# Latent attention of the decoded rows computed among the latents, inside the last pair's list

## The chip, the cores and the metric

The kernel runs on one core of one Trainium2 chip. A core has five engines with their own instruction queues: TensorE (PE: matrix products and transposes into PSUM), VectorE (DVE), ScalarE (ACT), GpSimd (POOL) and SyncE (SP, which here only starts DMAs). The metric is device time in microseconds, from the start of the program to its end. All arithmetic is to be exact to about single precision.

## The reference, cut to what matters

The program is one layer of an encoder with two attention branches, a gated merge and a convolutional feed-forward part, for a prompt of 1024 rows and, with the same weights, for 32 new rows of another sequence ("sample") that has a cache of 512 past rows. The change concerns branch A, the latent attention, of the sample alone:

```python
D_MODEL = 1024; SEQ = 1024; DEC_SEQ = 32; PAST_LEN = 512
H_A = 8; NOPE = 64; ROPE = 32; DV = 64; Q_RANK = 384; KV_RANK = 256

def expand_latent(c_kv, w_uk, w_uv):
    B, S, _ = c_kv.shape
    return (c_kv @ w_uk).reshape(B, S, H_A, NOPE), (c_kv @ w_uv).reshape(B, S, H_A, DV)

def mla_attend(q_nope, q_rope, qpos, k_nope, k_rope, v, kpos):
    s = (jnp.einsum('bqhd,bshd->bhqs', q_nope, k_nope)
         + jnp.einsum('bqhr,bsr->bhqs', q_rope, k_rope)).astype(jnp.float32) * MLA_SCALE
    mask = (kpos[None, :] // CHUNK) <= (qpos[:, None] // CHUNK)
    p = jax.nn.softmax(jnp.where(mask, s, NEG), axis=-1)
    return jnp.einsum('bhqs,bshd->bqhd', p.astype(v.dtype), v)

# for the sample:
    k_nope, v_a = expand_latent(jnp.concatenate([past_ckv, c_kv], axis=1), w_uk, w_uv)
    o_a = mla_attend(q_nope, q_rope, pos, k_nope, jnp.concatenate([past_krope, k_rope], axis=1), v_a, kpos)
```

So 544 latent rows of 256 numbers (512 cached, 32 new) are expanded to keys and values of 8 heads by 64, and each of 32 queries attends to all of them in each head. Since keys are latents times w_uk, the scores are also (query times the transpose of w_uk) times latents, and the output is also (weights times latents) times w_uv: both orders give the same numbers.

## The kernel before

The stages run in this order: normalisation and adaptive scales, branch B (stage_sb), the latents (stage_lat), branch A (stage_mla), the merge, the feed-forward part. Outside stage_mla's lists a scheduler of the framework decides at build time in which order the instructions of an engine stand.

Precision: most products are made of three (mm3, L70): both factors are split into a high and a low part of type float32r ("hi" on ACT, L64, "lo" on DVE, L67), and high x high, high x low and low x high are summed in PSUM. The sample's own attention uses plain float32 operands, one matmul each.

stage_mla (L1066) goes over four pairs of heads, p = 0 to 3. For each pair the prompt's attention follows a list written out by hand: ORDER_A (L639) for the first three pairs, ORDER_L (L671) for the last. mla_attend (L686) walks through the list, and the orders of PE, ACT and DVE are kept as written. A token names a step and a tile: S a score tile (PE, into one of three PSUM banks "s"), M its maximum (DVE), E the exponential (ACT), R and s the reciprocal of the sum (DVE), C and c the scaling by it (DVE, ACT), T the transposes of four 128x128 blocks of weights (PE, into one of two PSUM banks "tr"), h and v the split of them into high (ACT) and low part (DVE), V the product with the values (PE, bank "pv"), o and p its way out; f is one filler product of branch B's projection for the merge (three matmuls on PE, proj_b, L1421), G its store, W and w the split of its weights. In ORDER_A the letters I, i, x, y, z, X, J, j, Z, H, L expand the next pair's queries and keys (expansion, L1078). In ORDER_L, Y advances the sample's attention by one step, and q and r split a finished output of the pair.

The sample's attention goes in two halves of four heads, b = 0 and 1:

- mla_sample_load (L1329) loads a half's columns of w_uk and w_uv.
- mla_sample_keys (L1310) loads the cached latents, transposes them on PE (L1321) and splits them and the new ones into "PTh", "PTl", "CNh" and "CNl". It is called twice, before the second and before the third list.
- mla_sample_expand (L1334) splits the half's weights and makes its keys KSm and values VSm with mm3 (L72 to L74), with evictions on ACT (L1346, L1352). It runs before the second list for half 0 and before the third for half 1.
- mla_sample (L1355) makes the scores in two pieces of 272 keys (rotary part L1364, latent part L1367, for each two heads into 64 rows of the bank), softmax, transposes of the weights (L1388) and the sums with the values (L1396). Half 0 runs between the second and the third list, where the framework orders it; half 1 runs in the last list, at its 13 Y tokens. At its end POOL stores three of the four output tiles (L1403).

Behind the last list, L1289 loads the stored outputs "oa" of three pairs back (SP, into the buffers "big"), ACT and DVE split them, and the first products of w_proj_a with them (two PSUM groups for each 128 output columns, in the order of pairs 1, 2, 0) stand among the last list's own instructions on PE. Two tiles of w_proj_a are loaded into the memory of KSm (L1409).

Of the kernel before, what the change touches and what calls it, by code (L numbers as in the profile page):

```python
# [8 lines left out]
F32 = mybir.dt.float32  # L9
# [8 lines left out]
P = 128  # L18
# [26 lines left out]
class K:  # L45
# [582 lines left out]
    def sb_weights(self, pieces, w):  # L628
# [43 lines left out]
        S0.0 S0.1 S1.0 W f M0.0 f M0.1 M1.0 f E0.0 f E0.1 w S1.1 E1.0 G S2.0a R0.0 R0.1 R1.0 c0.0 M1.1 c1.0  # L672
        S2.0b f C0.1 E1.1 M2.0a f M2.0b T0.0 R1.1 f m2.0 C1.1 h0.0 S2.1a E2.0a v0.0 f E2.0b M2.1a S2.1b G s2.0
        R2.0 V0.0 c2.0 M2.1b S3.0a m2.1 o0 E2.1a T1.1 p0 T1.0 E2.1b M3.0a S3.0b h1.1 s2.1 R2.1 q S3.1a v1.1 h1.0
        r V1.1 v1.0 f C2.1 W f M3.0b V1.0 T2.2 w o1 T2.1 h2.2 p1 f m3.0 h2.1 M3.1a f q f v2.2 G f E3.0a v2.1
        T2.0 E3.0b V2.2 r h2.0 Y s3.0 R3.0 c3.0 v2.0 V2.1 Y V2.0 Y f o2 f2 p2 Y f2 G f Y q S3.1b G r S4.0a M3.1b
        Y M4.0a f Y m3.1 f E3.1a f Y f E3.1b S4.0b G s3.1 Y f R3.1 M4.0b f C3.1 Y m4.0 E4.0a T3.3 Y T3.2 E4.0b Y
        h3.3 s4.0 R4.0 h3.2 v3.3 c4.0 f v3.2 T3.1 Y f h3.1 S4.1a G v3.1 V3.3 M4.1a V3.2 V3.1 T3.0 S4.1b h3.0
        S5.0a v3.0 f M4.1b f V3.0 M5.0a f m4.1 o3 f E4.1a p3 G q S5.0b E4.1b r M5.0b S5.1a s4.1 m5.0 R4.1 E5.0a
        C4.1 E5.0b S5.1b M5.1a T4.3 s5.0 M5.1b T4.2 h4.3 R5.0 S6.0 m5.1 c5.0 v4.3 h4.2 M6.0 T4.1 E5.1a V4.3 v4.2  # L680
        h4.1 E5.1b V4.2 v4.1 E6.0 T4.0 s5.1 R5.1 V4.1 R6.0 C5.1 h4.0 S6.1 c6.0 v4.0 T5.2 M6.1 T5.1 h5.2 V4.0
        E6.1 v5.2 S7.0 o4 T5.0 R6.1 h5.1 M7.0 p4 S7.1 h5.0 C6.1 V5.2 v5.1 q E7.0 v5.0 T6.1 V5.1 r h6.1 V5.0 R7.0
        M7.1 c7.0 v6.1 T6.0 E7.1 o5 R7.1 h6.0 C7.1 p5 v6.0 q V6.1 r V6.0 T7.0 o6 h7.0 p6 v7.0 q r V7.0 o7 p7 q r
# [382 lines left out]
    def stage_mla(self):  # L1066
# [9 lines left out]
        Vs = None  # L1076

# [121 lines left out]
        for p in range(4):  # L1199
            if p == 1:  # L1200
                expanded = self.mla_sample_expand(M, raw, AB[1], *self.mla_sample_keys(M))
            if p == 2:
                cn = self.mla_sample_keys(M)
                Vs = values(1, raw, "mm")
                for _ in self.mla_sample(0, QZ, QR, *expanded):
                    pass
                proj["U"]()
                expanded = self.mla_sample_expand(M, raw_s, AB[1], *cn)
                proj["O"]()
# [14 lines left out]
            if p == 3:  # L1224

                v = self.tl(O, [P, 2 * T], F32R, "V")
                o3 = v[:, :T], v[:, T:]

                def split(o, r, c):
                    self.hi(o3[0][r, c], o[r])  # L1230
                    yield
                    self.lo(o3[1][r, c], o[r], o3[0][r, c])

                def out(*x):
                    parts.append(split(*x))

                parts, sample = [], self.mla_sample(1, QZ, QR, *expanded)
# [6 lines left out]
            def weights(k):  # L1244
                nonlocal raw, raw_s
                if k:
                    raw_s = self.mla_sample_load(1)
                elif p:
                    raw = load_values(1)
                else:  # L1250
                    raw = self.mla_sample_load(0)
# [3 lines left out]
            loads = iter(([expand, lambda: weights(0), U], [expand, lambda: weights(0), lambda: weights(1)],  # L1255
                          [expand, U, U, U], [])[p])
# [18 lines left out]
            raw_s = None  # L1275
# [34 lines left out]
    def mla_sample_keys(self, M):  # L1310

        nc, a = self.nc, self.a
        C = [[self.tl(self.At, [P, 512], F32R, g) for _ in range(2)] for g in ("PTh", "PTl")]
        N = [self.tl(M, [P, 2, TS], F32R, g, bufs=1) for g in ("CNh", "CNl")]
        cc = self.tl(self.At, [P, TP], F32, "A")
        nc.sync.dma_start(cc.rearrange("p (t c) -> p t c", t=4),
                          a["cache_mla_ckv"][0, 0].rearrange("(t p) c -> p t c", p=P))
        for k in range(2):
            tr = self.bank("tr")
            for t in range(4):  # L1320
                nc.tensor.transpose(tr[:, t * P : t * P + P], cc[:, t * 256 + k * P : t * 256 + k * P + P], self.idt)  # L1321
            self.hi(C[0][k], tr)
            self.lo(C[1][k], tr, C[0][k])
        new = self.CN.rearrange("p (k c) -> p k c", k=2)
        self.hi(N[0], new)
        self.lo(N[1], new, N[0])
        return C, [[x[:, k] for k in range(2)] for x in N]

    def mla_sample_load(self, b):  # L1329
        bc = slice(b * 256, b * 256 + 256)  # L1330
        return self.wload([(512 * i, 512, self.a[w][0, :, bc].rearrange("(k p) c -> p k c", p=P), 2)
                           for i, w in enumerate(("w_uk", "w_uv"))])

    def mla_sample_expand(self, M, raw, w, C, N):  # L1334

        nc = self.nc
        KSm = self.tl(M, [P, 2, KS], F32, "KSm")
        VSm = self.tl(M, [P, 5, 256], F32, "VSm")
        h, l = (x.rearrange("p (s k c) -> p s k c", s=2, k=2) for x in self.split_to(w, raw))
        for pp in range(2):  # L1340
            pc = slice(pp * P, pp * P + P)
            for (xh, xl), c0, n in ((C, 0, PAST), (N, PAST, TS)):
                ps = self.bank("mm")
                for k in range(2):
                    self.mm3(ps[:, :n], h[:, 0, k, pc], l[:, 0, k, pc], xh[k], xl[k], k == 0, k == 1)
                nc.scalar.copy(KSm[:, pp, c0 : c0 + n], ps[:, :n])  # L1346
        for t in range(5):
            (xh, xl), tk, r = (C, slice(t * P, t * P + P), P) if t < 4 else (N, slice(0, TS), TS)
            ps = self.bank("mm")
            for k in range(2):  # L1350
                self.mm3(ps[:r, :256], xh[k][:, tk], xl[k][:, tk], h[:, 1, k], l[:, 1, k], k == 0, k == 1)
            nc.scalar.copy(VSm[:r, t], ps[:r, :256])  # L1352
        return KSm, VSm

    def mla_sample(self, b, QZ, QR, KSm, VSm):  # L1355

        nc, vec = self.nc, self.nc.vector
        if b == 0:
            self.osm = self.sm2.tile([P, 4, TS], F32, name=self.nm("os"), tag="os", bufs=1)
        pieces = []  # L1360
        for j in range(2):
            c = slice(j * 272, j * 272 + 272)
            ps = self.tl(self.ps, [P, 512], F32, "s")
            nc.tensor.matmul(ps[:, :272], QR[64:128, 4 * b : 4 * b + 4].rearrange("p h q -> p (h q)"),  # L1364
                             self.KR[64:128, c], start=True, stop=False, skip_group_check=True)
            for pp in range(2):
                nc.tensor.matmul(ps[64 * pp : 64 * pp + 64, :272], QZ[:, 2 * b + pp], KSm[:, pp, c],  # L1367
# [934 lines left out]
```

## Time and profile before

| | us |
|---|---|
| median of 3 runs (1729.28 to 1729.77) | 1729.59 |
| the profiled execution's own time | 1731.46 |
| its span in the profile | 1729.6 |
| PE busy | 1691.4 |
| DVE busy | 1250.3 |
| ACT busy | 994.2 |
| POOL busy | 264.5 |

stage_mla's four lists lie roughly between 615 and 881 us of the span: the second begins at about 680, the third at about 747, the last at about 824.

How the rows are read. A row of the timeline is the start in us, the length in us, the engine, the line of the kernel, the operation, the tile written and the tiles read, shapes, and how many in a row; in brackets, the idle time of the engine ahead of it and what ended it. A row of the waits names the engine and line that waited, what it waited for, and the total in us, the number and the longest of these waits. A matmul's row on PE lasts until its result is out, while the next one is already running: what a matmul costs a busy PE is the step from its start to the next start, not its length. PEld rows are weight loads. Engine names with a q are their instruction queues (SPq issues DMAs).

### The profile page before, as it was taken

How to read it: one execution, taken by the hardware profiler on the slowest of the kernel's cores; microseconds unless marked ns; L12 is line 12 of the kernel's file. 1: busy time of each engine (PE TensorE's matmuls, PEld its weight loads, DVE VectorE, ACT ScalarE, POOL GpSimd, SP SyncE). 2: the span in 40 equal slices, each digit the busy share in tenths (PEclk: the TensorE clock that was granted, in tenths of full speed). 3: DMA queues.
4: the chain of work that ended last, by engine and by line, in shares of the span. 5: the costliest groups of instructions: out<-in, count | busy, mean ns of one | idle time of the engine just before them, and what ended most of it. 6: DMA issues, size and time to landing. Idle time of an engine off the chain costs nothing. (4 is left out here: it accounts for less than half of the span.)

```text
span 1729.6 us, 29836 instructions
## 1 busy us (share of the span) xinstructions
PE 1691.4 (98%) x11546; PEld 1542.1 (89%) x11546; DVE 1250.3 (72%) x2104; ACT 994.2 (57%) x1943; POOL 264.5 (15%) x513
## 2 busy tenths in 40 slices
PE   5999999999999999999999999999999999999998
PEld 3899999999999988989888789999999999977886
DVE  4596594693873587768785788887787787788456
ACT  4585594683872677767784276544444454544442
POOL 2211111111110011101100031111111121110013
PEclk8999999999999999999999999999999999999999
DMA  9343343333331222122245631534323323697743
GB/s 326 92 121 106 101 127 85 112 100 96 115 114 54 69 80 65 57 78 68 95 171 179 184 143 36 166 103 129 129 92 128 129 92 129 222 334 236 244 146 122
DMA packets 170142, 223.78 MB, mean 129 GB/s; under 512 B 12933, under 2 KB 117072, under 8 KB 170000
## 3 DMA queue, kind: packets, MB, share of 16 engines
q1 hardware_dynamic: 154336, 177.91, 32.6%
q0 software_dynamic: 15440, 43.88, 7.2%
q8 instruction: 91, 1.49, 0.4%
q14 instruction: 51, 0.42, 0.1%
q10 hardware_dynamic: 224, 0.09, 0.0%
HBM read 170.06 MB, written 51.25 MB: 128 GB/s over the span
## 5 line engine op out<-in xcount | busy, mean ns | idle before, releaser
L65 ACT ACTIVATE wh<-wr 128x1024 fp32r<-128x1024 f32 (+6 forms) x161 | 134.3, 844 | 252.4 <-PE s L1756 80.3
L68 DVE TENSOR_TENSOR wl<-wr,wh 128x1024 fp32r<-128x1024 f32 (+6 forms) x161 | 154.3, 966 | 144.2 <-ACT wh L65 144.1
L72 PE MATMUL mm<-hh,wh 128*128 128x352 f32 x696 | 232.0, 333 | 2.2 <-ACT nat L869 2.2
L73 PE MATMUL mm<-hl,wh 128*128 128x352 f32 x696 | 226.4, 325 | 0.0
L74 PE MATMUL mm<-hh,wl 128*128 128x352 f32 x696 | 225.7, 324 | 0.0
L72 PEld LDWEIGHTS mm<-hh,wh 128*128 128x128 f32 x696 | 131.4, 189 | 9.8 <-ACT nat L869 4.1
L73 PEld LDWEIGHTS mm<-hl,wh 128*128 128x128 f32 x696 | 131.4, 189 | 3.0 <-DVE hl L300 1.5
L74 PEld LDWEIGHTS mm<-hh,wl 128*128 128x128 f32 x696 | 131.3, 189 | 0.4 <-issue 0.4
L1757 PE MATMUL s<-T,wl 128*128 128x256 f32 (+1 forms) x328 | 93.6, 285 | 0.0
L1756 PE MATMUL s<-T,wh 128*128 128x256 f32 (+1 forms) x328 | 93.4, 285 | 0.0
L1755 PE MATMUL s<-T,wh 128*128 128x256 f32 (+1 forms) x328 | 93.3, 284 | 0.0
L1896 DVE SCALAR_TENSOR_TENSOR u<-u,c,u 128x1058 f32<-128x1058 f32 x68 | 87.0, 1316 | 1.9 <-ACT u L1893 0.7
L611 PE MATMUL tr<-c,A 128*128 128x128 f32 x576 | 83.3, 274 | 1.7 <-DVE PTl L68 0.8
L1755 PE MATMUL tr<-T,wh 128*128 128x272 f32 (+1 forms) x272 | 77.7, 286 | 0.0
L1757 PE MATMUL tr<-T,wl 128*128 128x272 f32 (+1 forms) x272 | 77.5, 285 | 0.0
L1756 PE MATMUL tr<-T,wh 128*128 128x272 f32 (+1 forms) x272 | 77.3, 284 | 0.0
L68 DVE TENSOR_TENSOR wl<-S,wh 128x1024 fp32r<-128x1024 f32 x40 | 48.9, 1223 | 36.7 <-ACT wh L65 36.7
L611 PEld LDWEIGHTS tr<-c,A 128*128 128x128 f32 x576 | 67.5, 140 | 8.5 <-DVE PTl L68 1.9
L68 DVE TENSOR_TENSOR PTl<-tr,PTh 128x512 fp32r<-128x512 f32 x100 | 67.1, 682 | 10.2 <-ACT PTh L65 9.8
L1757 PE MATMUL mm<-T,wl 128*128 128x256 f32 (+1 forms) x256 | 72.9, 286 | 0.3 <-DVE wl L68 0.2
L1755 PE MATMUL mm<-T,wh 128*128 128x256 f32 (+1 forms) x256 | 73.0, 286 | 0.0
L1756 PE MATMUL mm<-T,wh 128*128 128x272 f32 (+1 forms) x256 | 72.7, 284 | 0.0
(691 smaller groups left out, 5512.0 us busy)
## 6 DMA issues: line engine op xcount, KB each, us to landing
wr<-in_w_ada_dram SPq DMA_DIRECT2D x48, 512.0 KB, 4.5
wr<-in_w_up_dram SPq DMA_DIRECT2D x44, 512.0 KB, 4.4
dr<-in_w_down_dram SPq DMA_DIRECT2D x43, 512.0 KB, 5.7
wr<-in_w_in_dram SPq DMA_DIRECT2D x33, 512.0 KB, 4.8
wr<-gdn SPq DMA_DIRECT2D x30, 512.0 KB, 4.0
gdn<-u POOLq DMA_DIRECT2D x23, 512.0 KB, 5.0
gd<-nat POOLq DMA_DIRECT2D x48, 176.0 KB, 2.1
t<-gd SPq DMA_DIRECT2D x16, 528.0 KB, 5.2
```

The costliest lines, as they stand in the source:

```text
L65: self.nc.scalar.activation(out, in_, AF.Identity, scale=scale)
L68: return self.nc.vector.tensor_tensor(out, full, hi.bitcast(F32), ALU.subtract)
L72: m(ps, lh, rh, start=start, stop=False)
L73: m(ps, lh, rl, start=False, stop=False)
L74: self.pe = m(ps, ll, rh, start=False, stop=stop).ins
L611: self.nc.tensor.transpose(tr[:, (2 * s + q) * P : (2 * s + q + 1) * P], at[q][:, b * P : b * P + P], self.idt)
L1755: m(ps[:, :n], w[0][:, k], x[0][:, k, c], start=first and k == 0, stop=False, skip_group_check=True)
L1756: m(ps[:, :n], w[0][:, k], x[1][:, k, c], start=False, stop=False, skip_group_check=True)
L1757: i = m(ps[:, :n], w[1][:, k], x[0][:, k, c], start=False, stop=k == 3, skip_group_check=True)
L1896: nc.vector.scalar_tensor_tensor(y, u[:, w : w + YW], self.cvT[:, w, cc : cc + 1], y, ALU.mult, ALU.add)
```

## The change

The keys and values of the sample are no longer expanded. The sample's attention runs entirely in the last list:

- KSm now holds the transposed latents and VSm the latents themselves. VSm is loaded once, at the beginning of stage_mla; mla_sample_latents, called before the second list, fills KSm by ten transposes on PE, two evictions on ACT and two copies on DVE.
- mla_sample makes both halves in one generator. It loads the whole w_uk and w_uv, as float32, into two of the three buffers "big" and uses the third for the turned w_uk. Two groups of four transposes turn w_uk; one group of eight matmuls makes the queries among the latents. Each half then makes its scores, softmax and transposes as before, sums latents (256 numbers for each of 128 query rows), evicts the sums, multiplies them by w_uv and copies the result out. All these groups use "tr" banks.
- ORDER_L is a new order of the same steps, with 32 Y tokens in place of 13. ORDER_A is the same.
- The calls between the lists and the loads inside them that served the expansion are dropped; values (the prompt's values of the second two pairs, before the third list) uses banks "mm" and "tr" in turn in place of "mm" alone.
- Two output tiles are stored after half 0 and one after half 1, in place of three after half 1.

```diff
     ORDER_L = """
-        S0.0 S0.1 S1.0 W f M0.0 f M0.1 M1.0 f E0.0 f E0.1 w S1.1 E1.0 G S2.0a R0.0 R0.1 R1.0 c0.0 M1.1 c1.0
...
+        S0.0 S0.1 S1.0 W f M0.0 f M1.0 f M0.1 E0.0 f E1.0 w f E0.1 Y G S1.1 R0.0 R1.0 R0.1 Y C0.1 S2.0a c0.0
+        c1.0 M1.1 S2.0b M2.0a E1.1 Y M2.0b T0.0 Y R1.1 f m2.0 C1.1 S2.1a h0.0 E2.0a v0.0 f E2.0b Y M2.1a s2.0
...
+        T5.2 M6.1 S7.0 h5.2 Y f E6.1 R6.0 M7.0 T5.1 v5.2 c6.0 f R6.1 C6.1 h5.1 T5.0 V5.2 E7.0 v5.1 h5.0 S7.1 G
...
+        self.KSm = self.tl(M, [P, 2, KS], F32, "KSm")
+        self.VSm = self.tl(M, [P, 5, 256], F32, "VSm")
+        nc.sync.dma_start(self.VSm[:, :4], a["cache_mla_ckv"][0, 0].rearrange("(t p) c -> p t c", p=P))
...
             if p == 1:
-                expanded = self.mla_sample_expand(M, raw, AB[1], *self.mla_sample_keys(M))
+                self.mla_sample_latents()
             if p == 2:
-                cn = self.mla_sample_keys(M)
-                Vs = values(1, raw, "mm")
-                for _ in self.mla_sample(0, QZ, QR, *expanded):
-                    pass
+                Vs = values(1, raw, "mm tr")
                 proj["U"]()
-                expanded = self.mla_sample_expand(M, raw_s, AB[1], *cn)
                 proj["O"]()
...
-                parts, sample = [], self.mla_sample(1, QZ, QR, *expanded)
+                parts, sample = [], self.mla_sample(QZ, QR)
...
+    def mla_sample_latents(self):
+        nc = self.nc
+        KSm, VSm = self.KSm, self.VSm
+        new = self.CN.rearrange("p (k c) -> p k c", k=2)
+        nc.vector.tensor_copy(KSm[:, :, PAST:], new)
         for k in range(2):
             tr = self.bank("tr")
             for t in range(4):
+                nc.tensor.transpose(tr[:, t * P : t * P + P], VSm[:, t, k * P : k * P + P], self.idt)
+            nc.scalar.copy(KSm[:, k, :PAST], tr)
+        tr = self.bank("tr")
+        for k in range(2):
+            nc.tensor.transpose(tr[:TS, k * P : k * P + P], new[:, k], self.idt)
+        nc.vector.tensor_copy(VSm[:TS, 4], tr[:TS, :256])
+
+    def mla_sample(self, QZ, QR):
...
+        WT, WV, X = (self.tl(self.At, [P, BIG], F32, "big") for _ in range(3))
+        for x, w in ((X, "w_uk"), (WV, "w_uv")):
+            nc.sync.dma_start(x[:, :1024].rearrange("p (k c) -> p k c", k=2),
+                              self.a[w][0].rearrange("(k p) c -> p k c", p=P))
+        def steps():
+            for b in range(2):
+                tr = self.bank("tr")
+                for pp in range(2):
+                    for k in range(2):
+                        c = k * 512 + b * 256 + pp * P
+                        nc.tensor.transpose(tr[:, pp * 256 + k * P : pp * 256 + k * P + P], X[:, c : c + P], self.idt)
+                yield
+                nc.scalar.copy(WT[:, b * 512 : b * 512 + 512], tr)
+                yield
+            tr = self.bank("tr")
+            for b in range(2):
                 for k in range(2):
+                    for pp in range(2):
+                        c = b * 512 + pp * 256 + k * P
+                        o = b * 256 + k * P + pp * 64
+                        nc.tensor.matmul(tr[:, o : o + 64], WT[:, c : c + P], QZ[:, 2 * b + pp], start=True, stop=True,
+                                         skip_group_check=True)
+            yield
+            nc.scalar.copy(X[:, :512], tr)
+            yield
+            for b in range(2):
+                yield from half(b)
+        def half(b):
+            Qs, o = X[:, b * 256 : b * 256 + 256], X[:, 512 + b * 256 : 768 + b * 256]
...
+                for k in range(2):
+                    nc.tensor.matmul(ps[:, :272], Qs[:, k * P : k * P + P], KSm[:, k, c],
+                                     start=False, stop=k == 1, skip_group_check=True)
...
+            tr = self.bank("tr")
             for k in range(2):
+                for kt in range(5):
+                    r = P if kt < 4 else TS
+                    nc.tensor.matmul(tr[:, k * P : k * P + P], VSm[:r, kt, k * P : k * P + P], PT[:r, kt * P : kt * P + P],
+                                     start=kt == 0, stop=kt == 4)
+            yield
+            nc.scalar.copy(o, tr[:, :256])
+            yield
+            tr = self.bank("tr")
             for pp in range(2):
+                for k in range(2):
+                    c = k * 512 + b * 256 + pp * P
+                    nc.tensor.matmul(tr[:, pp * 64 : pp * 64 + 64], WV[:, c : c + P],
+                                     o[:, k * P + pp * 64 : k * P + pp * 64 + 64], start=k == 0, stop=k == 1)
             yield
             for h in range(2):
+                x = tr[64 * h : 64 * h + 64, :P].rearrange("p (q c) -> p q c", q=2)
+                vec.tensor_copy(osm[64 * h : 64 * h + 64, 2 * b : 2 * b + 2], x[:, :, 32 * h : 32 * h + 32])
+            for k in ((0, 1), (2,))[b]:
+                nc.gpsimd.dma_start(self.oad[k][:, TP:T], osm[:, k])
             yield
```

More of the change, by code (lines that the diff above doesn't have):

```diff
@@ L677 @@
[L677 to L681, printed above, removed]
@@ L1320, in mla_sample_keys @@
             for t in range(4):
[L1321 to L1332, printed above, removed]
```

133 lines of the change are left out of this document (47 added, 86 removed).

## The prediction

> **What bounds the kernel now.** I read the page's head first, then TensorE's waits, then the busy time in the stretches of the last three head pairs, then single rows of the timeline.
>
> ```profile
> span 1729.6 us, 29836 instructions
> PE 1691.4 (98%) x11546; PEld 1542.1 (89%) x11546; DVE 1250.3 (72%) x2104; ACT 994.2 (57%) x1943; POOL 264.5 (15%) x513
> PEclk8999999999999999999999999999999999999999
> ```
>
> TensorE (PE) works 98% of the span at the full granted clock; the next engine, VectorE (DVE), 72%. So what the change takes off PE comes off the end, unless PE then has to wait. The stretch of the last pair, where the edit puts its work (length; then PE, weight loads, DVE, ScalarE (ACT) and POOL busy; clock, DMA share, GB/s):
>
> ```profile
> 824.00:881.00 57.00, 55.19 (x384) 47.05 (x383) 45.85 (x114) 43.80 (x110) 4.95 (x10) 1.00 0.31 111
> ```
>
> DVE and ACT are busy 80% and 77% there and the DMA engines 31%: they have room, and PE lacks 1.8 of 57 us. TensorE's longest waits from 600 to 900 us, over all four pairs (total, times, longest), are few:
>
> ```profile
> PE mm L72 <- DVE KL L68: 1.4, 1, 1.4
> PE s L1216 <- ACT A L719: 1.0, 4, 0.3
> PE tr L611 <- DVE PTl L68: 0.8, 2, 0.4
> ```
>
> **What the change removes from PE.** A busy time of PE counts overlapping ends, so I price by steps from start to start.
>
> ```profile
> 855.16 0.49 PE L611 MATMUL tr<-c,A 128*128 128x128 f32 x3
> ```
>
> ```profile
> 679.41 0.93 PE L1321 MATMUL tr<-c,A 128*128 128x128 f32 x7
> ```
>
> Three transposes last 0.49 us and seven 0.93: a step is 0.11. The two calls of mla_sample_keys have 16: 1.8 us.
>
> ```profile
> 684.60 0.39 PE L73 MATMUL mm<-PTl,wh 128*128 128x512 f32 x1
> 684.83 0.39 PE L74 MATMUL mm<-PTh,wl 128*128 128x512 f32 x1
> ...
> 685.31 0.26 PE L72 MATMUL mm<-CNh,wh 128*128 128x32 f32 x1
> 685.42 0.26 PE L73 MATMUL mm<-CNl,wh 128*128 128x32 f32 x1
> ...
> 687.03 0.28 PE L73 MATMUL mm<-wl,PTh 128*128 128x256 f32 x1
> 687.15 0.28 PE L74 MATMUL mm<-wh,PTl 128*128 128x256 f32 x1
> ```
>
> Each of the two expansions has 12 products of 512 columns (2 blocks, 2 k, 3 products) at 0.23, 12 of 32 columns at 0.11, and 30 of 256 (5 row tiles, 2 k, 3) at 0.12: 2.76 + 1.32 + 3.60 = 7.7; both 15.4 us.
>
> The old attention itself, of a half: two score pieces, five transposes, ten sums matmuls. A matmul of plain fp32 is two passes in the trace.
>
> ```profile
> 844.53 0.72 PE L1364 MATMUL s<-lat,QRm 64*128 64x272 f32 x2
> 845.18 0.68 PE L1367 MATMUL s<-KSm,QZ 128*64 128x272 f32 x4
> 845.79 0.39 PE L625 MATMUL pv<-PTh,V 128*128 128x256 f32 x1
> ```
>
> A piece takes 1.26: 0.65 for the rotary part, 0.61 for two matmuls on 64 columns each, which run side by side. Before the third pair the scheduler split one such pair, and one matmul alone cost 0.60:
>
> ```profile
> 747.78 0.67 PE L1367 MATMUL s<-KSm,QZ 128*64 128x272 f32 x2
> 748.38 0.38 PE L72 MATMUL mm<-wh,lat 128*128 128x256 f32 x1
> ```
>
> So four pieces are 3 x 1.26 + 0.65 + 2 x 0.60 = 5.6. Ten transposes: 1.1. Of the sums, five matmuls (ten passes) take
>
> ```profile
> 855.48 1.36 PE L1396 MATMUL pv<-A,VSm 128*128 128x64 f32 x10
> 856.78 0.39 PE L72 MATMUL mm<-ObH,wh 128*128 128x264 f32 x1
> ```
>
> 1.30, and there are four such groups: 5.2. **Removed: 1.8 + 15.4 + 5.6 + 1.1 + 5.2 = 29.1 us.**
>
> **What it adds to PE.** Transposes: 10 in mla_sample_latents, 8 of w_uk, 10 of weights: 28 x 0.11 = 3.1. Queries through the turned w_uk and sums through w_uv: 8 matmuls each of 64 columns, the form of the sums row, 16 x 0.26 = 4.2. Sums of latents: again 4 groups of five, but 128 columns wide. The row knows only 64 columns; below, weight loads bound it and the price stays 1.30; above, doubled columns double it to 2.60. A 256-column product above already steps at 0.12, so columns are not what bounds these passes; I take 1.40: 5.6. Scores: 4 pieces of one rotary part (0.65) and two matmuls with all 128 columns, so nothing runs side by side. The trace has one plain fp32 matmul of that width, with 352 columns:
>
> ```profile
> 594.27 0.86 PE L928 MATMUL mm<-big,c 128*128 128x352 f32 x2
> 594.70 0.59 PE L73 MATMUL s<-hl,wh 128*128 128x352 f32 x1
> 595.13 0.32 PE L74 MATMUL s<-hh,wl 128*128 128x352 f32 x1
> ```
>
> From 594.27 to 595.13, less the 0.16 that a 352-column product takes by the steps above, is 0.70; for 272 columns 0.54. Bounds of a new piece: 1.26, if two matmuls in one accumulation hide as the old pair did, and 1.95, at the rotary part's 0.65 each. I take 0.65 + 2 x 0.575 = 1.80, between the 0.54 and the 0.60 of the single matmul: 7.2. **Added: 3.1 + 4.2 + 5.6 + 7.2 = 20.1. PE's balance: -9.0 us**, from -11.6 (cheap ends of sums and pieces) to -3.6 (dear ends).
>
> [...]
>
> **ACT, DVE, DMA.** They lose more than they get: two splits of 1024 weights, four splits and 18 evictions go; two evictions before the lists and, in the last list, three of 128x512 and two of 128x256 come, with one half's two exponentials and two copies: nine instructions, at most 0.59 each (the 512-column eviction quoted under (d)), some 5 us on ACT, and fewer on DVE. That list has 57 - 43.8 = 13 us of idle ACT, so this costs nothing as long as PE's list stays long; if that cover were gone, it would cost those 5 us. SP loses six loads and gets three. The latents (VSm) are issued behind a w_proj_b load and wait for a PE matmul of the stage before, that is over before the load behind it can go, so nothing queues. The whole w_uk and w_uv wait for buffers that the third list frees long before. No term.
>
> **What PE waits for instead.** The expansions were filler at the heads of the second and third list, while the first weights go through maximum, exponential and scaling. The last list had no such filler, and shows the price of its absence:
>
> ```profile
> 827.33 0.28 PE L74 MATMUL mm<-ObH,wl 128*128 128x264 f32 x1
> 827.95 0.50 PE L1216 MATMUL s<-KH,QH 128*128 128x512 f32 x1 [0.34 <-ACT A L719]
> ...
> 830.49 0.28 PE L74 MATMUL mm<-ObH,wl 128*128 128x264 f32 x1
> 831.33 0.44 PE L611 MATMUL tr<-c,A 128*128 128x128 f32 x2 [0.55 <-DVE A L726]
> ```
>
> The steps are 0.62 and 0.84 where 0.12 is normal: 1.2 us lost. I charge 1.2 to each of the second and the third list (bounds 0, if DVE, relieved of the splits, comes that much earlier, and 3): +2.4. Waiting there are the fourth score tile for a bank of "s", and behind it on PE the whole list. In the last list the turning of w_uk (two Y steps of four transposes, 0.44 each) now stands just ahead of these two waits: -0.8.
>
> Last, the end of half 1 moves later, and the loads of oa behind it. Now the chain is:
>
> ```profile
> 854.77 0.39 DVE L1400 COPY os<-pv 64x32 f32<-64x32 f32 x2
> ...
> 862.54 1.09 ACT L65 ACTIVATE KH<-big 128x1056 fp32r<-128x1056 f32 x1 [0.94 <-DMA big<-oa]
> ...
> 865.42 0.32 PE L72 MATMUL mm<-KH,wh 128*128 128x352 f32 x1
> ```
>
> 10.7 us from the copy to the product that needs it. In the built program's order PE has, between the last step of half 1 and that product, 21 transposes, 15 products on ObH and ObL, 20 value products, two score tiles of three products and six products of 352 columns: at the steps above 2.3 + 1.8 + 2.4 + 0.8 + 1.0 = 8.3 us, between 9 and 10 with the breaks at changes of form. I charge +0.6 (bounds 0 and 2). **Sum: -9.0 + 2.4 - 0.8 + 0.6 = -6.8 us.** The profiled execution took 1731.46 us (span 1729.6 and 1.9 around it), so 1724.7; it lies 1.9 above the median of 1729.59, so the forecast is 1722.8.
>
> **Rivals.** (a) The heads of the lists need no filler and the order of the last list is better throughout: 2.4 and 0.6 go, and 1 us of its other waits: -10.8, 1718.8. For it: the waits on ACT at L1216 lie mostly in that list. Against: the two steps just shown. 0.22.
>
> (b) Wide passes are dear: sums groups at 2.0 and pieces at 1.95, +3.0: 1725.8. For it the rotary part's 0.65; against, the 0.54. 0.13.
>
> (c) The end of half 1 comes too late: the chain of 10.7 finds half of its cover, because other waits shift the list: +5, no change of note, 1727.8. For it: a chain of five engines; against: over 8 us of work stand in the order. [...] 0.10.
>
> (d) Slower: the two "tr" banks. Eleven sample groups in the last list now hold one of them until ACT has copied it, and a T tile of the list that comes meanwhile waits for the other, whose own release is a chain of
>
> ```profile
> L65 ACT ACTIVATE PTh<-tr x16: 577/593/611, 680.5 to 747.5; 128x512 fp32r<-128x512 f32 x16
> L68 DVE TENSOR_TENSOR PTl<-tr,PTh x16: 679/684/692, 681.2 to 748.9; 128x512 fp32r<-128x512 f32 x16
> ```
>
> 0.59 + 0.68 = 1.3 us. All eleven: +14, 1737. It decides from eight on (+10.4: slower by 0.2%). For it: PE waits at L611 for PTl already now; against: most Y steps stand where no T does. 0.06.
>
> **How the numbers follow.** The forecast has 0.49, and 1720 to 1725.5 as its own range. 1722.8 is its time. The range for 8 in 10 runs from 1717.0, below (a), to 1727.8, at (c); beyond lie (d), half of (c) and a tail of (a). A measurement of this kernel can tell 0.2% (3.5 us) from no change, so faster means under 1726.1: nearly all of the forecast, (a), half of (b): 0.79. Within: half of (b), (c): 0.15. Slower: (d): 0.06.
>
> **What would show it.** L1321 and the products on PTh and CNh are gone; the new scores' piece lasts 1.8 and five sums of latents 1.4; PE waits for ACT at L1216 and for DVE at the first transposes at the heads of the second and third list, 1.2 each; the head of the third list moves earlier by some 6 us, that of the last by 20, and the last list lasts some 13 longer than its 57. Wrong would make it: a PE wait over 2 us for KH or for a "tr" bank, or sums of latents at twice their old time.

## The result, and the profile after

The changed kernel takes 1719.47 us in the median (6 runs, 1717.07 to 1720.6), the kernel before 1729.68 beside it (6 runs, 1728.32 to 1730.7): 10.2 us less by the medians. The ratio given with these runs is 0.9932 with the interval 0.9922 to 0.9942 (10.0 to 13.5 us), so the medians stand near its upper end. The forecast was 1722.8, and 6.8 us less: the measured time lies in its range for 8 in 10, but 0.5 us below its own band of 1720 to 1725.5, near the 1718.8 of rival (a). The profiled execution has this head:

```profile
span 1717.1 us, 29638 instructions
PE 1680.4 (98%) x11472; PEld 1533.0 (89%) x11472; DVE 1246.3 (73%) x2094; ACT 987.6 (58%) x1924; POOL 269.9 (16%) x513
```

PE is still the bound and is busy for 11.0 us less. Of its waits from 600 to 900 us the one for KL, ahead of the first list, is as it was, those for ACT at the scores have the same sum in fewer places, and those for PTl, 0.8 us before, are no longer in the list. The two longest are now:

```profile
PE mm L72 <- DVE KL L68: 1.4, 1, 1.4
PE s L1216 <- ACT A L720: 1.0, 2, 0.6
```

To see where they went, both executions are cut at the same products. The stretches are: the end of the first list, the stage ahead of the second, the second list, the stage ahead of the third (with that list's first three score tiles, which the framework set among the stage's work), the third list, the last list up to a product on V behind it, and the rest. First before, then after (length; then busy time and instructions of PE, weight loads, DVE, ACT, POOL; clock, DMA share, GB/s):

```profile
664.00:674.27 10.27, 9.70 (x69) 8.80 (x68) 9.81 (x23) 7.71 (x20) 1.07 (x2) 1.00 0.48 130
674.27:690.20 15.93, 15.62 (x106) 14.08 (x104) 10.52 (x23) 9.60 (x23) 1.04 (x2) 1.00 0.08 21
690.20:740.63 50.43, 49.83 (x363) 45.80 (x362) 38.78 (x97) 37.78 (x96) 8.11 (x14) 1.00 0.26 82
740.63:769.60 28.97, 28.63 (x190) 24.19 (x189) 19.25 (x46) 16.84 (x42) 2.14 (x4) 1.00 0.23 61
769.60:827.33 57.73, 57.67 (x415) 53.17 (x414) 43.45 (x109) 41.34 (x100) 9.11 (x16) 1.00 0.19 60
827.33:887.21 59.88, 58.04 (x400) 49.87 (x399) 47.12 (x118) 45.71 (x117) 4.88 (x9) 1.00 0.29 105
887.21:1729.60 842.39, 831.49 (x5674) 756.14 (x5673) 637.89 (x862) 412.23 (x639) 136.24 (x284) 1.00 0.47 157
```

```profile
663.04:672.52 9.48, 9.48 (x69) 8.85 (x68) 9.02 (x21) 7.45 (x18) 1.07 (x2) 1.00 0.20 57
672.52:680.67 8.15, 8.03 (x54) 7.04 (x52) 5.41 (x14) 4.92 (x8) 1.04 (x2) 1.00 0.07 16
680.67:731.08 50.41, 50.31 (x363) 45.95 (x362) 41.65 (x104) 38.63 (x101) 8.09 (x14) 1.00 0.22 71
731.08:744.16 13.08, 12.89 (x91) 11.92 (x90) 10.41 (x23) 7.46 (x15) 1.04 (x2) 1.00 0.25 71
744.16:802.99 58.83, 58.17 (x416) 53.32 (x414) 47.38 (x119) 44.18 (x109) 9.14 (x16) 1.00 0.23 72
802.99:873.72 70.73, 69.30 (x477) 60.22 (x475) 51.91 (x125) 50.98 (x128) 6.55 (x19) 1.00 0.27 97
873.72:1717.10 843.38, 832.53 (x5675) 756.12 (x5673) 636.36 (x860) 411.23 (x638) 141.02 (x276) 1.00 0.47 157
```

| stretch | change, us | the forecast's terms there |
|---|---|---|
| all ahead of the first cut | -1.0 | 0 |
| end of the first list | -0.8 | 0 |
| ahead of the second | -7.8 | -7.7 - 0.9 + 1.1 = -7.5 |
| second list | 0.0 | +1.2 |
| ahead of the third | -15.9 | -7.7 - 0.9 - 6.2 = -14.8 |
| third list | +1.1 | +1.2 |
| last list and tail | +10.9 | +13.3 - 0.8 + 0.6 = +13.1 |
| attention in all | -12.5 | -6.8 |
| the rest | +1.0 | 0 |

The attention has the first six stretches, without what lies ahead of them. Each of these came out a little better than its terms. They repeat well: in a second profile of the kernel before (below) each list takes the same to 0.1 us, and in a second one of the changed kernel's PE program (the run with all stores late) one wait alone differs, some 0.7 us at 844 us, which is in the +10.9 here. The other two rows are less sure. The second profile of the kernel before is also 1.0 us earlier at the first cut, and has 841.0 us in the rest where the first has 842.4. So neither of the two rows can be read as an effect from one pair of profiles. But in all the profiles below the rest takes 841.7 to 844.6 us in the changed kernel and its variants (eleven), and 841.0 to 842.4 in the kernel before and its one variant (three). A loss of one or two us behind the attention is therefore likely; its cause was not looked for.

In the last list the prices of the new products can be read row by row:

```profile
809.05 1.89 PE L1347 MATMUL tr<-QZ,big 128*128 128x64 f32 x16
810.75 0.72 PE L625 MATMUL pv<-ptd,V 128*128 128x256 f32 x4
...
814.99 0.72 PE L1361 MATMUL s<-lat,QRm 64*128 64x272 f32 x2
815.65 1.18 PE L1364 MATMUL s<-KSm,big 128*128 128x272 f32 x4
816.47 0.48 PE L625 MATMUL pv<-PTh,V 128*128 128x256 f32 x1
...
817.55 0.72 PE L1361 MATMUL s<-lat,QRm 64*128 64x272 f32 x2
818.20 1.19 PE L1364 MATMUL s<-KSm,big 128*128 128x272 f32 x4
819.23 0.60 PE L611 MATMUL tr<-c,A 128*128 128x128 f32 x4
...
827.84 2.97 PE L1393 MATMUL tr<-A,VSm 128*128 128x128 f32 x20
830.74 0.47 PE L1216 MATMUL s<-KH,QH 128*128 128x448 f32 x1
```

From start to next start: eight matmuls for queries 1.70 us (0.106 for each pass), a score piece 1.48 us (0.66 for the rotary part, 0.82 for four passes of the latent part) or, where transposes follow, 1.68, the sums of a half 2.90 (1.45 for each group of five).

And the end of the first list, before and then after, the same place with nothing of the sample's in it but a split of weights:

```profile
661.69 1.06 ACT L65 ACTIVATE wh<-wr 128x1024 fp32r<-128x1024 f32 x1 [0.17 <-PE mm L73]
662.78 1.23 DVE L68 TENSOR_TENSOR wl<-wr,wh 128x1024 fp32r<-128x1024 f32 x1 [0.44 <-ACT wh L65]
663.92 0.68 DVE L68 TENSOR_TENSOR PTl<-tr,PTh 128x512 fp32r<-128x512 f32 x1
664.75 0.41 PE L611 MATMUL tr<-c,A 128*128 128x128 f32 x2 [0.40 <-DVE PTl L68]
```

```profile
660.73 0.63 ACT L65 ACTIVATE wh<-wr 128x512 fp32r<-128x512 f32 x1 [0.17 <-PE mm L73]
663.24 0.60 PE L611 MATMUL tr<-c,A 128*128 128x128 f32 x4
```

Before, ACT and DVE stood in a split of 1024 columns, PTl came late, and PE waited for the bank; after, the split there has 512 columns, PTl comes 0.8 us sooner against the same products (at 662.16), and the wait is gone.

### The profile page after: what moved, and what is told of

Same layout as the page of the kernel before. It is cut to its first block, busy times and chain, and to the rows that moved or that the text cites. A ratio compares the mean times of both kernels' runs of the same rounds, so it can differ in the third digit from the quotient of the medians.

```text
span 1717.1 us, 29638 instructions
## 1 busy us (share of the span) xinstructions
PE 1680.4 (98%) x11472; PEld 1533.0 (89%) x11472; DVE 1246.3 (73%) x2094; ACT 987.6 (58%) x1924; POOL 269.9 (16%) x513
```

## The experiments

**The splits put back.** Loads and splits of the sample weights as they were, results unused.

```diff
+            if p in (1, 2):
+                self.split_to(AB[1], raw_s)
             if p == 1:
                 self.mla_sample_latents()
```

> The changed kernel with the two loads and splits of sample weights of 1024 columns put back where they were, their results unused. Theory A: ACT and DVE do these splits at the ends of the first two lists, in front of the evictions of transposed weights, and PE waited there: in the trace of before the steps into L611 and into the ptd products are 0.56 and 0.33 us too long at 664 and 672 us, and the same two places of the second list lost 0.54 and 0.24; in the changed kernel they are gone. Putting the splits back then costs 0.56 + 0.33 + 0.54 + 0.24 = 1.7 us and the waits on PTl at L611 are in the trace again (bounds 1.0 to 2.5). Rival B: these waits were chance in one execution, or hang on the expansions' products and not on the splits: the time stays within 0.3 us and no wait on PTl over 0.2 us appears.

Measured: 1720.02 us (5 runs, 1718.36 to 1721.4), ratio to before 0.9944 (0.993 to 0.9957). PE's waits from 600 to 900 us have, beside those of the changed kernel, again

```profile
PE tr L611 <- DVE PTl L68: 0.8, 2, 0.4
```

At the four places the steps are longer than in the changed kernel by 0.56 and 0.24 (first list), 0.56 and 0.22 us (second): 1.6. Theory A holds in the trace: from the first cut to 840 us this kernel loses 2.1 us against the changed one. The spans are equal all the same (1717.2 and 1717.1), because the changed kernel's profile has the wait at 844 us, which this one lacks, and a longer rest. The medians differ by 0.55 only, which their spread (3 us) neither contradicts nor shows.

**The values on two banks.** One edit undone.

```diff
-                Vs = values(1, raw, "mm tr")
+                Vs = values(1, raw, "mm")
```

> The changed kernel with the values of the second half taken through the two mm banks alone, as before the change, and not through mm and tr in turn. My forecast had no term for this edit. Theory A: the four value tiles ahead of the third list follow each other without anything between them, and with two banks the third waits until ACT and DVE have evicted the first (two evictions of 256 columns, about 0.4 us each on each engine): +0.3 to +1.5 us, seen as PE waiting in the L72 to L74 products ahead of the third list. Rival B: products of the list's head or of w_proj_b fill in, 0 +- 0.3 us.

Measured: 1722.02 (5 runs, 1719.41 to 1722.74), ratio 0.9953 (0.994 to 0.9965): 2.5 us more, above theory A's 1.5. PE's waits that are new or larger:

```profile
PE mm L72 <- DVE V L68: 1.3, 3, 0.8
PE mm L72 <- DVE sum L725: 1.3, 1, 1.3
```

The first line is theory A's; the second is a filler product in the third list's head. The profile puts its wait down to DVE; that it comes from the later values is likely, not shown. The choice of banks is thus worth some 2.5 us here: without it the lost filler ahead of the third list would have cost that much.

**A later tail.** The last two steps of half 1 moved down the list.

```diff
-... M6.0 q Y r E6.0 T5.2 M6.1 S7.0 h5.2 Y f E6.1 ... v5.1 h5.0 S7.1 G R7.0 v5.0 T6.1
+... M6.0 q r E6.0 T5.2 M6.1 S7.0 h5.2 f E6.1 ... v5.1 h5.0 Y S7.1 G R7.0 Y v5.0 T6.1
```

> The changed kernel with the last two steps of half 1 (sums through w_uv, copies and store of os) put some 14 and 16 instructions groups later in the last list, about 4 to 5 us of PE's work. Theory A (rival c of the forecast, the chain os copy, store, load of oa, split of KH, product): the chain takes 8.57 us in the changed kernel, from the copy at 857.45 to the product at 866.02, and the product starts 0.29 us after the split of KH has ended, so there is no slack left; a delay of 4 to 5 us is paid with 2 to 5 us, as PE's waits for KH or QH after the last list. Rival B: products on the other two K tiles of oa, which no longer wait for half 1 (two of its three column tiles are stored at the end of half 0), and the last list's own products take the place: under 1 us.

Measured: 1720.53 (5 runs, 1719.03 to 1721.67), ratio 0.9945 (0.9933 to 0.9958). The copy of os came at

```profile
862.28 0.46 DVE L1407 COPY os<-tr 64x64 f32<-64x64 f32 x2 [1.13 <-PE tr L1402]
```

some 3.8 us later than in the changed kernel, counted from the last common product; 1.5 us of that were paid, in two short waits, for a tr bank (0.5) and for KL (0.2), and in breaks. It lies between both theories, nearer to B.

**No sample steps in the last list.**

```diff
-                parts, sample = [], self.mla_sample(QZ, QR)
+                parts, sample = [], iter(range(32))
+                ...
+                nc.gpsimd.memset(osm, 0.0)
```

> The changed kernel with all the sample steps of the last list left out (the sample rows of oa are zeros), mla_sample_latents and everything else kept. The steps' own PE time in the trace of the changed kernel, from first to last start of each group, sums to 17.3 us without the 0.42 us that one of them waits. Theory A: PE's time is the price, and the steps stand in nobody's way: -17.3 us, or up to 0.8 less where a list head loses the eight transposes of w_uk as filler: -16.5 to -17.3. Rival B (rival d of the forecast: the tr banks held by the steps make T tiles wait, or the tail waits for half 1): more than -18.5 us. Rival C: steps that fill stalls are free in part: less than -15 us.

Measured: 1709.78 (4 runs, 1709.48 to 1710.51), ratio 0.9884 (0.9871 to 0.9898): 9.7 us less than the changed kernel, not 17.3. Rival C. The last list's stretch, and PE's longest waits from 800 to 890 us:

```profile
803.87:864.99 61.12, 52.40 (x360) 45.44 (x359) 46.87 (x107) 45.68 (x110) 4.99 (x16) 1.00 0.25 88
```

```profile
PE s L1216 <- ACT A L720: 3.4, 3, 2.4
PE tr L611 <- DVE A L727: 2.5, 3, 1.2
```

PE is busy 52.4 of 61.1 us where it was busy 69.3 of 70.7. Without the steps, PE comes too early for the softmax of the prompt's weights: it waits for the exponentials (ACT, L720) and for the scaled weights (DVE, L727).

**The same with the old order.** ORDER_L of before, its 13 Y tokens empty.

> As the run without sample steps (1709.8 us), but the last list in the order of before, its 13 sample steps left out too. That run gave 9.7 us where the steps hold 17.3 of PE, and PE waited 11 us in the last list, up to 2.6 at a time, for weights (A) still being scaled. Theory A: it is the order that waits, since it was laid out around 32 sample steps; the old order, laid out around 13 with 5.5 us of PE, stands nearer to a list without any: PE waits 4 to 7 us there, and the time is 1703 to 1706. Rival B: without the sample steps DVE and ACT bound the list whatever the order: 1709 to 1711.

Measured: 1706.6 (4 runs, 1705.1 to 1708.24), ratio 0.9865 (0.9852 to 0.9879), 0.6 us above theory A's range:

```profile
804.77:862.89 58.12, 54.07 (x363) 47.37 (x362) 44.43 (x107) 43.82 (x110) 4.34 (x8) 0.97 0.28 95
830.70:834.10 3.40, 3.34 (x15) 3.13 (x16) 2.15 (x5) 3.25 (x7) 0.00 (x0) 0.51 0.10 39
```

3.0 us of the stretch come back by the order alone, and the list is 1.8 us shorter than the 59.9 it took before with half 1 in it, whose groups hold 5.5 us of PE (two pieces at 1.26, five transposes, two groups of sums at 1.3). But this profile has a loss of its own: behind two waits of 1.5 and 0.8 us the granted clock was 0.51 for 3.4 us (second line), and these hold what would be some 1.7 us at the full clock (3.40 x 0.51, an estimate). Without this the list would be some 3.5 us shorter, so about 2 of the 5.5 us of sample work in the old list were free, as filler. Two of the four runs, 1705.1 and 1705.57, lie in theory A's range; whether they were spared the slower clock, no trace shows.

**The sums twice.** What more PE work costs in the new list.

```diff
-            for k in range(2):
+            for k in (0, 0, 1, 1):
                 for kt in range(5):
```

> The changed kernel with the sums of latents of both halves computed twice over (the second time starts the bank anew, same results): 40 more passes on PE at the 0.145 us that they step in its trace, 5.8 us. Theory A: PE bounds the last list, and what is added there is paid in full: +5.8 (5.0 to 6.2), 1725.3. Rival B, from the run without the sample steps: the list has stalls that more PE work only fills (2.9 us of steps too long are left in it): +3 to +4.5.

Measured: 1725.46 (6 runs, 1723.74 to 1725.65), ratio 0.997 (0.9959 to 0.9981): 6.0 us more. Each of the two groups now takes 5.90 us instead of 2.90:

```profile
828.00 5.97 PE L1393 MATMUL tr<-A,VSm 128*128 128x128 f32 x40
833.90 0.48 PE L1216 MATMUL s<-KH,QH 128*128 128x448 f32 x1
```

Theory A: with all the sample work in it, the list has no free room left at these places, and what is added there is paid in full.

**The expansions' products left out of the kernel before.**

```diff
         self.split_to(w, raw)
+        nc.gpsimd.memset(KSm, 1.0)
+        nc.gpsimd.memset(VSm, 1.0)
-        ... the products of both loops and their evictions
```

> The kernel before with the products of both expansions and their evictions left out (keys and values of the samples are ones); the loads, the splits, the transposes of mla_sample_keys and both halves stay. The products take 2 x 7.7 = 15.4 us of PE. Theory A (the forecast's charge): the head of the second list loses filler worth 1.2 us, that of the third keeps half 0: -14.2. Theory B, formed after the run with the values on two banks: ahead of the third list the products also covered the evictions of the value tiles, 2.1 us and more there without them, so -15.4 + 1.2 + 2 = -12.2. Rival C: no stall takes their place: -15.4 or more.

Measured: 1716.79 (4 runs, 1715.3 to 1717.6), ratio 0.9925 (0.991 to 0.994): 13.2 us less than the 1730.04 beside it, between A and B. The head of the second list has a new wait:

```profile
PE s L1216 <- ACT A L719: 1.4, 1, 1.4
```

That is the forecast's lost filler, and it costs more than the 1.2 charged. In the changed kernel the score tile at this place (682.49 us) doesn't wait at all; the head loses 0.8 further on, in breaks, that is steps that are longer than usual without a wait of note. What this kernel keeps there and the changed one drops, are the splits: of the weights, which by themselves cost the head nothing net when they were put back, and of the latents (two of 512 columns on each of ACT and DVE). That it is the latter was not tried by itself. Ahead of the third list no stall of the values shows; half 0 is still there as cover, so B's second term fails.

**The rotary part over 128 rows.**

```diff
-QR[64:128, 4 * b : 4 * b + 4] ... self.KR[64:128, c]
+QR[:, 4 * b : 4 * b + 4] ... self.KR[:, c]
+        nc.gpsimd.memset(QR[0:64], 0.0)
+        nc.gpsimd.memset(self.KR[0:64], 0.0)
```

> The changed kernel with the rotary part of the sample scores taken over all 128 rows (rows 0 to 63 of KR and QRm set to zero once), not over rows 64 to 127. In the trace of the changed kernel its two passes step 0.33 and 0.32 us, and the four passes of the latent part, over 128 rows and as many columns, 0.33, 0.23, 0.23 and 0.03 to 0.23. Theory A: a pass over 64 rows costs more than one over 128, because its weights can't be loaded beside the pass before: with 128 rows both passes step 0.23, and the first latent one too: a piece falls from 1.47 to 1.67 us by 0.3, four of them by 1.2 us, the time to 1718.3. Rival B: the 0.32 is the cost of the first passes into a new bank of s, whatever the rows: no step changes, same time.

Measured: 1717.88 (5 runs, 1717.83 to 1718.94), ratio 0.9932 (0.9919 to 0.9944), where the runs of before were 1730.04. The same piece in the timeline:

```profile
815.01 0.62 PE L1363 MATMUL s<-lat,QRm 128*128 128x272 f32 x2
815.47 1.08 PE L1366 MATMUL s<-KSm,big 128*128 128x272 f32 x4
816.19 0.48 PE L625 MATMUL pv<-PTh,V 128*128 128x256 f32 x1
```

1.18 us instead of 1.48, and all passes step 0.23; four pieces give 1.2. Theory A holds in the trace. The time alone doesn't show it: a run that is in effect the changed kernel once more (the one with all stores late, below) has 1718.19. The weight loads show how the piece gets shorter. In the changed kernel, then in this one:

```profile
814.99 0.29 PEld L1361 LDWEIGHTS s<-lat,QRm 64*128 64x128 f32 x2
815.64 0.76 PEld L1364 LDWEIGHTS s<-KSm,big 128*128 128x128 f32 x4 [0.36 <-issue]
```

```profile
814.89 0.31 PEld L1363 LDWEIGHTS s<-lat,QRm 128*128 128x128 f32 x2
815.24 0.88 PEld L1366 LDWEIGHTS s<-KSm,big 128*128 128x128 f32 x4
```

With one shape the loads of the latent part start while a rotary pass still runs (815.24 against 815.47). Where the shape changes from 64 rows to 128, the load starts at 815.64, only as the matmul itself does (815.65): it isn't hidden. The first load of the rotary part shows the same: over 64 rows it starts at 814.99, with its matmul (814.99), over 128 at 814.89, ahead of its matmul (815.01).

**The same, with filler in the last list's head.**

```diff
-M2.0b T0.0 Y R1.1 f m2.0 C1.1 S2.1a h0.0 E2.0a v0.0 f E2.0b
+M2.0b f T0.0 Y R1.1 m2.0 C1.1 f S2.1a h0.0 E2.0a v0.0 E2.0b
```

> The rotary part over 128 rows, and in the last list's head one group of w_proj_b products ahead of the first transposes and one ahead of the fourth score tile, each moved up by some places. PE waits there 0.42 us (for the scaled A) and 0.60 us (for ACT's exponentials) in the changed kernel. Theory A: a group is 0.36 us of PE's work and fills as much of each wait: 0.6 to 0.7 us less than with the rotary part alone, 1717.2. Rival B: what the two groups leave behind opens as waits for V0.0 or for the next score bank: no gain, 1717.9 or up to 0.4 more.

Measured: 1716.98 (5 runs, 1715.97 to 1719.54), ratio 0.992 (0.9905 to 0.9935). In the trace the wait at the transposes (0.3 by the list of waits) is gone, the one for ACT stays at 0.4: half of what A expected. The medians of both variants lie under the changed kernel's 1719.47; the filler's share can't be told from chance by times.

**All three stores behind half 1.**

```diff
-            for k in ((0, 1), (2,))[b]:
+            for k in ((), (0, 1, 2))[b]:
```

> The changed kernel with all three stores of the samples' rows of oa at the end of half 1, as before the change (there two of them go at the end of half 0). The products after the list take the column tiles of oa in the order 1, 2, 0. In the run with a late tail they began with tile 1, 8 us before the load of tile 2 had been split, and only 1.5 us of a delay of 4 us were paid. Theory A: the early store of tiles 0 and 1 is what gives PE work while tile 2 is under way; without it all three loads start behind half 1, as at 860 us now, and the first product on QH comes no earlier than that on KH, at about 866: +1 to +4 us, seen as PE's waits for QH, KH or KL behind the last list. Rival B: the value products and scores left in the list cover the chain as they did before the change (10.7 us, no wait): 0 +- 0.5.

Measured: 1718.19 (5 runs, 1717.4 to 1720.26), ratio 0.9929 (0.9916 to 0.9942). The question stays open, because POOL's order is the framework's and not the list's: the first two stores stood at 833.7 us all the same (834.1 in the changed kernel), and PE's instructions are the changed kernel's one for one. In the kernel before, too, two of the three went early (761.9 and 764.0), and not all three behind half 1 as the list of the change has it: in this the change altered nothing. So this is in effect the changed kernel run again, and its median shows what chance does: 1.3 us. What late stores would cost wasn't tried.

**The kernel before once more.**

> The kernel before, unchanged, for a second profile of it. The first one had PE waits at the ends of the first two lists (0.56 and 0.33, then 0.54 and 0.24 us) and stood 1.8 us above the median of its runs. Theory A: the waits belong to the kernel and come again within 0.2 us each; the 1.8 us lie elsewhere, in the loading ahead of 40 us and the stages after the attention. Rival B: the waits are chance and at least two of the four are gone.

Measured: 1728.72 us. The waits at the list ends are there again (PTl 0.8 us in 2, ptd 0.4 in 2), as theory A has it. The rest behind the attention took

```profile
885.91:1726.90 840.99, 831.53 (x5674) 756.19 (x5673) 637.67 (x862) 412.17 (x639) 138.86 (x284) 1.00 0.47 157
```

1.4 us less than in the first profile, by the same instructions; the other 1.3 us between the two spans lie ahead of the second list.

**The tail later still.** Both steps behind C7.1 and h6.0.

```diff
...
-T6.0 C7.1 o5 f p5 h6.0 f q
+T6.0 C7.1 o5 Y f p5 h6.0 Y f q
```

> The changed kernel with the last two steps of half 1 later still: behind C7.1 and behind h6.0, some 8 us of PE's work after their place in the changed kernel (the run with a late tail had moved the copy of os by 3.8 us and stood 1.5 us behind at the end of the attention in its trace). Theory A (rival c with a threshold): products on tile 1 of oa, whose samples' row is stored with half 0, and products on V and the next weights fill what they can; what is beyond some 3 us is paid in full, so a copy at about 866 costs 4 to 6 us, with PE waiting for KH or KL over 2 us at one place. Rival B: no threshold, the list's tail always finds other work: under 2 us.

Measured: 1724.35 (5 runs, 1722.54 to 1725.68), ratio 0.9961 (0.9947 to 0.9974): 4.9 us more than the changed kernel. One wait, and the clock behind it:

```profile
PE mm L72 <- ACT KH L65: 4.1, 1, 4.1
```

```profile
869.00:873.00 4.00, 0.27 (x3) 0.06 (x1) 1.22 (x3) 1.53 (x3) 0.13 (x2) 0.80 0.98 346
873.00:878.00 5.00, 4.62 (x15) 4.41 (x16) 3.65 (x3) 3.34 (x4) 0.39 (x6) 0.50 1.02 413
```

The copy of os came at 865.19, 7 us later counted from the last common product. Of the first 4 us of delay other work takes most, as the run with a later tail showed; beyond that PE stands still (4.1 us), and then works at half the clock (0.50 until about 878 us). Theory A.

## Why the prediction was right, point by point

**The balance of PE: right in kind, the saving 1.9 us too small.** What goes, 29.1 us, was priced from its own rows. What comes was priced at 20.1 and measured at some 18.2. The score pieces took 2 x 1.48 + 2 x 1.68 = 6.3, not 7.2: the step that failed priced an unpaired matmul by the one half-array matmul in the trace (0.60) and by a 352-column one (0.70 for two passes), though a pass over the whole array steps only 0.23. The products with w_uk and w_uv took 1.70 + 2 x 0.84 = 3.4, not 4.2: their price came from a group with a block of 32 rows in it, whose change of shape was in the mean (from 856.21 to 856.42 us into that block, a step of 0.2, and as much out of it, where the others have 0.11). The sums of latents took 5.8 for 5.6, as the chosen value between 1.30 and 2.60 had it. So rival (b), dear wide passes, falls.

**The heads of the lists: right in kind.** The third list lost 1.1 us for the 1.2 charged. The second lost 0.8 and got them back at its end (next point); with the products alone gone, the wait there was 1.4, so the charge was near the full price. That the relief of DVE, which the forecast had named as the reason for its bound of 0, removed this wait in the changed kernel is likely and was not tried by itself. For the last list's head the forecast gave back 0.8 for the turning of w_uk; the two waits there went from 0.50 + 0.72 to 0.60 + 0.42 us in steps, so 0.2.

**ACT and DVE, "No term": wrong, 1.6 us.** The forecast quoted PE's waits for PTl (0.8 us) and called the removed splits free because ACT and DVE have room. On average they have; at the ends of the first two lists the splits of 1024 columns stood ahead of evictions that PE needed next. Putting them back brought the waits back, and a second profile of before has them too.

**The values' banks: no term, and none needed, but for a reason that the forecast didn't see.** Work between the values' products (half 0 and the expansion) did more than cover weights in the list's head: it also covered the evictions of the values. With the expansions' products alone gone, half 0 was cover enough. On "mm" alone that would have cost 2.5 us, about the upper bound of 3 set on a head's loss.

**The tail and rival (c): no cost, and (c) priced.** 0.6 was charged, and no wait for KH or its like was paid:

```profile
857.45 0.45 DVE L1407 COPY os<-tr 64x64 f32<-64x64 f32 x2
...
864.65 1.08 ACT L65 ACTIVATE KH<-big 128x1056 fp32r<-128x1056 f32 x1
...
866.02 0.33 PE L72 MATMUL mm<-KH,wh 128*128 128x352 f32 x1
```

8.6 us lie between copy and product, about the cover that the forecast counted, and the product finds KH 0.3 us old. The two runs with a later tail show where (c) begins (a delay of 4 us, 1.5 paid) and that its 5 us were the right size for a delay of 7; some 2.3 us of these are the clock of 0.50, an estimate from the products' steps (0.29 us where 0.16 is usual). Rival (d) did not come: no T tile waits for a "tr" bank that the sample holds.

**Which case it was.** Rival (a), nothing lost at the heads or the tail, had 1718.8, which is nearer to the measured time than the forecast; but the reasons differ from its own: the third head did lose. What the new order of the last list gives by itself, with the same work in it, was not tried. With the corrections of 1.9 (prices), 0.4 (second head), 1.6 (splits) and 0.6 (tail), less 0.6 at the last head, the forecast's -6.8 becomes -10.7, inside the interval of the ratio. All but one of these lie on the same side, so the direction was safe while the size was off by a third. Of the 12.5 in the attention 1.8 are left, 1.1 of them ahead of the third list; there the framework had set single score products of half 0 between products of other shapes, and breaks at changes of shape are the likely cause, which was not tested. One sum of the forecast does not come out: its chance of a faster kernel, 0.79, is at most 0.775 by its parts (0.49 + 0.22 + half of 0.13).

Of the signs that the forecast named, the waits of 1.2 us at the heads of the second and third list came at the third alone, 0.8 us for ACT. In the timeline the first score tile of the third list stands 14.4 us earlier (6 forecast: the sign left out the scores of half 0, which stood ahead of that tile), that of the last 24.4 (20), and the last list is 10.9 longer (13). No PE wait over 2 us for KH or a "tr" bank came, and the sums did not double.

## What to carry to other kernels

An engine with room on average can still be late at one place: look for what stands in its queue just ahead of the instruction that the bound engine waits for, before a split or copy is called free. Work that moves into a list costs less than its own time as long as it fills stalls of that list, and all of it from there on; leaving work out of a tuned order, on the other hand, measures the order as well as the work. A price for a matmul belongs to its shape on the array, and a change of shape belongs in it (0.30 of the 1.48 us of a score piece here).

## What the runs showed of the hardware

Mixing shapes of the array in one accumulation had a price in these runs: two passes of 272 columns over 64 rows followed by four over 128 took 1.48 us, all six over 128 rows (with zeros in half the rows of the first two) 1.18. The weight load after the change of shape started only with its own matmul (815.64 and 815.65 us); with one shape it started 0.23 us ahead of it.

Two matmuls side by side on 64 columns each had taken 0.61 us for four passes behind such a rotary part over 64 rows, about as much as one of them alone (0.60, two passes); the four whole passes that replace them take 0.82 there, and 0.72 behind passes of their own shape. But the 0.60 has a change of shape ahead of it and behind it, and two passes over the whole array step 0.46 among their like. So the pairs that the change gave up had saved 0.1 to 0.2 us a piece and not the half.

In two runs the granted clock was halved behind waits of PE. In the run with the tail later still PE stopped at 869.3 us for 4.1 us; the clock was 1.00 from 870 to 871 us, 0.71 from 871 to 872 and 0.50 from 872 until about 878, and products of 352 columns stepped 0.29 us where 0.16 is usual. That came on top of the wait, some 2.3 us by these steps. In the run without sample steps and in the old order the clock was 0.51 from 830.7 to 834.1 us, behind waits of 1.5 and 0.8 us, which cost some 1.7 us. In the run without sample steps a wait of 2.4 us left the clock full (1.00 in its stretch). So the length of one wait doesn't tell these runs apart; what decides it was not shown.
